# Differential heads: ScalarE copies the four banks, and each head rotates and splits in its lane

## The chip, the cores and the metric

One NeuronCore of a Trainium2 chip runs the whole program in one launch. The metric is the device time of one execution in microseconds (us). Five engines work side by side and meet through semaphores: TensorE (PE) multiplies into the eight banks of PSUM, VectorE (DVE) and ScalarE (ACT) read PSUM and SBUF, GpSimd (POOL) reads SBUF alone, and SyncE (SP) starts transfers from HBM.

## The reference

Two layers of a decoder trunk on 512 tokens of width 2048, in float32. A layer normalises its input, projects it by `w_in`, runs three groups of attention heads beside each other, gates each, and projects the 2048 joined outputs by `w_out`. The change touches the differential heads, of which a layer has four:

```
qa = apply_rope(a_q.reshape(B, S, 4, 2, 64), cos, sin)
ka = apply_rope(a_k.reshape(B, S, 4, 2, 64), cos, sin)
va = a_v.reshape(B, S, 4, 128)
p = softmax(causal(q k^T * 64 ** -0.5))          # two score maps a head
a = p[:, :, 0] - lam * p[:, :, 1]
y_a = rms_norm(a @ va, subln_w, 1e-5) * (1 - lam_init)

apply_rope(x): [x1 * cos - x2 * sin, x2 * cos + x1 * sin]   # halves of 32
```

## The kernel before

Every float32 operand of a large product is split into a rounded part and a remainder (names with `hi`, `h` and `lo`, `l`), and a product is three matmuls: hi by hi, hi by lo, lo by hi. A weight tile of 128 rows comes by DMA into `raw`, ACT rounds it to `whi`, and POOL (during the stages that matter here) subtracts to get `wlo`; there are four slots for such pairs.

A GEMM runs over 16 such tiles (`sweep`), with the four token blocks of 128 in the four PSUM banks `g`. Tiles 0 and 1, and tiles 14 and 15, are taken together, bank by bank; the others one at a time, bank by bank too. Of the differential heads each has a GEMM of its own, with 384 columns (keys 128, queries 128, values 128); a tile of it is 12 matmuls. The next head's GEMM writes the same four banks again.

Attention runs in two **lanes** (class `Lanes`), generators that issue a piece of a head's work after each tile of the GEMM that runs then; a `yield` of a number lets that many modelled microseconds of PE work pass first. `L_SPLIT` is 2.6, `L_ROWS` 3.0, `L_DA` 4.5, `L_RSQRT` 4.0. PE executes in exactly the order in which the program issues; the instructions of the other engines are put in an order by a scheduler at build time, and each engine then keeps to it. `lanes.finish(task)` issues what is left of a task at once, with no GEMM tile between its pieces.

The steps of a head (`da_head`) are, by the names of its tiles: transposes `qT` and `kT` of the rotated queries and keys, scores `sc` for 1, 2, 3 and 4 blocks of keys (shapes 128x128 to 128x512, two maps each), softmax on DVE and ACT into `p`, transposes `pT` of it, products `oT` with the split values `vh`, `vl`, then the norm: column sums `css` on PE, an inverse square root in 11 small DVE instructions (`rsq_u`, `rsub`), its split (`rh`, `rl`) onto two diagonal tiles `dh`, `dl`, and a product `R` on PE that spreads them. A lane has two PSUM banks for all of these in turn.

In the kernel before, the code between two heads' GEMMs reads the banks directly. For each of the four blocks DVE multiplies keys and queries by sine and cosine (`rope`, three instructions that read the bank), adds (two instructions; the keys are written twice, the second time by an ACT copy), ACT writes `vh`, and DVE `vl`, both from the bank. The tables `rtabs` hold sine and cosine already multiplied by the row's norm factor `r_in`.

I call the code after the GEMM of the first, second, third and fourth head boundary 1, 2, 3 and 4 of a layer.

Of the kernel before, what the change touches and what calls it, by code (L numbers as in the profile page):

```python
# [12 lines left out]
F32 = mybir.dt.float32  # L13
F32R = mybir.dt.float32r
I32 = mybir.dt.int32
AF = mybir.ActivationFunctionType
ALU = mybir.AluOpType
AX = mybir.AxisListType

P = 128  # L20
S = 512
NB = S // P
# [86 lines left out]
def trunk(ctx: ExitStack, tc: tile.TileContext, ins, inv_freq, out):  # L109
# [12 lines left out]
    def slot(name, tag, dt=F32, shape=(P, S)):  # L122
        return w2.tile(list(shape), dt, name=name, tag=tag, bufs=SLOTS[tag])
# [7 lines left out]
    lanes = Lanes()  # L131
    V = nc.vector
    A = nc.scalar
# [14 lines left out]
    def split(hi, lo, src, scale=None, behind=False, E=V):  # L148

        if scale is None:  # L150
            late(A.copy(hi, src), behind)  # L151
            E.tensor_tensor(lo, src, hi.bitcast(F32), op=ALU.subtract)  # L152
        else:
            late(A.activation(hi, src, AF.Copy, scale=scale), behind)
            E.scalar_tensor_tensor(lo, src, scale, hi.bitcast(F32), op0=ALU.mult, op1=ALU.subtract)  # L155
# [35 lines left out]
    tabs = [const.tile([P, NB, 64], F32, name=n) for n in ("cos", "sin")]  # L191
# [41 lines left out]
    def rope(dst, src, m, heads, tables, dup=0):  # L233


        co, si = tables
        n, z = heads * 64, dup * 64
        t = slot("rope", "et")
        u = t[:, n:2 * n] if dup else dst
        t = t[:, 0:n]  # L240
        sv, tv, uv = (x.rearrange("p (h d) -> p h d", d=64) for x in (src, t, u))
        V.tensor_tensor(tv[:, :, 0:32], sv[:, :, 32:64],  # L242
                        si[:, m:m + 1, 0:32].broadcast_to([P, heads, 32]), op=ALU.mult)
        V.tensor_tensor(tv[:, :, 32:64], sv[:, :, 0:32],
                        si[:, m:m + 1, 32:64].broadcast_to([P, heads, 32]), op=ALU.mult)
        V.tensor_tensor(uv, sv, co[:, m:m + 1, :].broadcast_to([P, heads, 64]), op=ALU.mult)
        if dup:
            dv = dst[:, 0:2 * z].rearrange("p (h u d) -> p h u d", u=2, d=64)
            V.tensor_tensor(dv[:, :, 0, :], uv[:, 0:dup, :], tv[:, 0:dup, :], op=ALU.add)
            A.copy(dv[:, :, 1, :], dv[:, :, 0, :])  # L250
        if dup < heads:
            V.tensor_tensor(dst[:, 2 * z:], u[:, z:], t[:, z:], op=ALU.add)

    def scaled_tables(r, half, to):

# [99 lines left out]
    def stack_q(lane, tag, tok_tiles, c0):  # L355

        t = bank("qT", lane)
        for m in range(NB):
            transpose(t[:, m * P:(m + 1) * P], tok_tiles[m][:, c0:c0 + P])
        e, o = slot("qe", tag, F32R), slot("qo", tag, F32R)  # L360
        A.copy(e[0:64], t[0:64])
        A.copy(o[64:128], t[64:128])
        V.tensor_tensor(e[64:128], t[0:64], e[0:64].bitcast(F32), op=ALU.subtract)
        V.tensor_tensor(o[0:64], t[64:128], o[64:128].bitcast(F32), op=ALU.subtract)
        return e, o

    def dup_k(lane, tok_tiles, c0, tag="k"):

        t = bank("kT", lane)
        for m in range(NB):  # L370
            transpose(t[:, m * P:(m + 1) * P], tok_tiles[m][:, c0:c0 + P])
        hi, lo = slot("kh", tag, F32R), slot("kl", tag, F32R)
        split(hi, lo, t)
        return hi, lo
# [158 lines left out]
    def layer(l, pre, norms, r_in, start=None):  # L533
# [41 lines left out]
        rtabs = [slot(n, "rtab", shape=(P, NB, 64)) for n in ("rcos", "rsin")]  # L575
        qt = [[None] * NB for _ in range(2)]
        keys = []
        for half in range(2):
            ms = (2 * half, 2 * half + 1)
            ps = gemm_tok(act_block, w_in, [(C_KR, 64), (B_K, 256)], 320, ms=ms,  # L580
                          before=lambda k: fed(half, k))
# [3 lines left out]
            kd = []  # L585
            for t_ps, m in zip(ps, ms):
                d = slot("kd", "rot")
# [6 lines left out]
            if half == 0:  # L594
                c = layer_constants(l)
            ps = gemm_tok(act_block, w_in, [(B_Q, 512)], 512, ms=ms)
# [86 lines left out]
        def spread_r(lane):  # L683
            V.tensor_tensor(r_sq, r_in, r_in, op=ALU.mult)
            d = diagonals(r_in, f"pT{lane}")
            yield L_SPLIT
            t = bank("R", lane)
            spread(t, d)
# [6 lines left out]
        ps = gemm_tok(act_block, w_in, [(B_Q + 512, 512)], 512)  # L695
# [25 lines left out]

        qscale = layer_c.tile([P, NB], F32, name=f"qscale{l}")
        kvscale = layer_c.tile([P, NB], F32, name=f"kvscale{l}")
        R = slot("R", "R")

        def kv_scale(lane, ssum):
            yield L_SPLIT
# [2 lines left out]
            yield L_SPLIT  # L730
            t = bank("R", lane)
            spread(t, d)
            A.copy(R, t)

# [4 lines left out]
        ps = gemm_T(act, w_in, [(C_Q, S)])  # L739
        qh, ql, ssum = latent(ps, c["qnw"])  # L740
        scales = [lanes.add(q_scale, ssum)]
        ps = gemm_T(act, w_in, [(C_KV, S)])
# [4 lines left out]
        ps = gemm_tok(lambda k, m: cut((qh[k], ql[k]), m), w_uq, [(192 * h + 128, 64) for h in range(4)], 256, nk=4)  # L747
        qr = []
        for m in range(NB):
            d = slot("qr", "rot")  # L750
# [11 lines left out]
        for ps in gemm_T(lambda k: (qh[k], ql[k]), w_uq, [(192 * h, 128) for h in range(4)], nk=4):  # L762
            t = (slot("qnh", "gy", F32R), slot("qnl", "gy", F32R))
# [3 lines left out]
        def up_kv(pr, ready):  # L767
# [20 lines left out]
            for j in range(2):  # L788
                t = (slot("knh", "k", F32R), slot("knl", "k", F32R))
                kf = slot("kf", "et")  # L790
                V.tensor_tensor(kf, ps[j], R, op=ALU.mult)
                split(t[0], t[1], kf)
# [6 lines left out]
        def mla_head(lane, h, kn, vv):  # L799
# [3 lines left out]
            for i in range(NB):  # L803
# [8 lines left out]
                if i == 1:  # L812
                    yield L_ROWS
            yield L_MLA
# [4 lines left out]
        kn, vv = up_kv(0, scales + stacks)  # L819
        heads = [lanes.add(mla_head, h, kn, vv) for h in (0, 1)]  # L820
        gate_chunk(C_G, 12)
        kn, vv = up_kv(1, heads)
# [6 lines left out]
        stage = [0] * 5  # L829
        heads_out = [None] * 4  # L830

        def da_head(lane, h, rot, vv):
            yield L_SPLIT
            yield lambda: h == 0 or stage[h - 1] >= 2
            qq = stack_q(lane, f"qE{lane}", rot, 256)
            kk = [dup_k(lane, rot, 0)]
            yield L_SPLIT
            kk.append(dup_k(lane, rot, 128))
            stage[h] = 1
            yield L_SPLIT  # L840
            probs = prob_slots(lane)
            for i in range(NB):
                n = (i + 1) * P
                cc = slice(i * P, (i + 1) * P)
                p1 = slot("p", f"p{lane}")[:, 0:n]
                recs = []
                for u in range(2):
                    t = bank("sc", lane)
                    mm(t[:, 0:n], qq[u][:, cc], kk[u][0][:, 0:n], start=True, stop=False)
                    mm(t[:, 0:n], qq[u][:, cc], kk[u][1][:, 0:n], start=False, stop=True)  # L850
                    recs.append(softmax_rows((probs[i], p1)[u], t[:, 0:n], n, causal[:, S - n:S], 64.0 ** -0.5))
                V.tensor_tensor(recs[1], recs[1], c["nlam"], op=ALU.mult)
                V.tensor_scalar(probs[i], probs[i], recs[0], None, op0=ALU.mult)  # L853
                V.scalar_tensor_tensor(probs[i], p1, recs[1], probs[i], op0=ALU.mult, op1=ALU.add)  # L854
                if i < 3:
                    yield L_ROWS
            stage[h] = 2
            yield L_DA
            o = yield from causal_AV(lane, probs, lambda b: (vv[0][:, b, :], vv[1][:, b, :]))
            sq = slot("sq", f"p{lane}")  # L860
            heads_out[h] = slot("on", "gy")
            A.activation(sq, o, AF.Square)
            A.activation(heads_out[h], o, AF.Copy, scale=c["sub"])
            yield L_ROWS
            ms = sm("ms")
            V.tensor_scalar(ms, col_sums(bank("css", lane), sq), 1.0 / 128, SUB_EPS, op0=ALU.mult, op1=ALU.add)
            d = diagonals(rsqrt(ms, "rsub"), f"pT{lane}")
            yield L_RSQRT + L_SPLIT
            t = bank("R", lane)
            spread(t, d)  # L870
            V.tensor_tensor(heads_out[h], heads_out[h], t, op=ALU.mult)

        das = []
# [4 lines left out]
        for h in range(4):  # L878
            ps = gemm_tok(
                act_block, w_in, [(A_K + 128 * h, 128), (A_Q + 128 * h, 128), (A_V + 128 * h, 128)], 384)  # L880
            if h == 0:
                lanes.finish(*heads)
            if h > 0:
                lanes.finish_until(lambda: stage[h - 1] >= 1)
            if h > 1:
                lanes.finish(das[h - 2])
            rot = []
            vv = (slot("vh", "v", F32R, (P, NB, P)), slot("vl", "v", F32R, (P, NB, P)))
            for m in range(NB):
                d = slot("da_rot", "rot")  # L890
                rope(d[:, 0:384], ps[m][:, 0:256], m, 4, rtabs, dup=2)
                rot.append(d)
                split(vv[0][:, m, :], vv[1][:, m, :], ps[m][:, 256:384], r_in[:, m:m + 1])
            das.append(lanes.add(da_head, h, rot, vv))

        gate_chunk(A_G, 0, lambda k: split_y(k) if k >= 4 else None)

# [65 lines left out]
    r_in = layer_c.tile([P, NB], F32, name="r_in0")  # L963
# [25 lines left out]
    for l in range(1, DEPTH):  # L989
# [1 line left out]


SLOTS = {"gy": 16, "kr": 2, "p0": 4, "p1": 4, "pT0": 2, "pT1": 2, "qE0": 2, "qE1": 2, "k": 4, "v": 4,
         "rot": 6, "rtab": 2, "et": 3, "R": 1, "Rin": 1}
N_RAW = 3
N_SPLIT = 4
L_SPLIT = 2.6
L_ROWS = 3.0
L_SW = 5.0
L_MLA = 7.0  # L1000
L_DA = 4.5
# [29 lines left out]
```

## Time and profile before

| | |
|---|---|
| three runs | 1814.95, 1817.13, 1818.06 us (median 1817.13) |
| profiled execution | 1818.91 us, of which the span of instructions is 1817.1 us |
| PE busy | 1744.7 us, 96% of the span |
| DVE, ACT, POOL busy | 900.4, 816.7, 784.6 us |
| mean granted clock of PE | 0.985 of full speed |

PE is busy nearly all the time, and the matmuls of the program are the floor. What another engine does costs time only where PE waits for it, or where the clock of PE is granted at the lower of its two levels (0.5, that is 1.2 GHz in place of 2.4).

### The profile page before, as it was taken

The page shows a single profiled execution, that of the slowest core. Times are in us where ns is not written, and L with a number is a line of the kernel's source. Part 1 is how long each engine was busy: PE and PEld are TensorE (multiplying, and loading weights), DVE is VectorE, ACT ScalarE, POOL GpSimd, SP SyncE. Part 2 cuts the span into 40 slices and gives each one's busy share as a digit, 9 for nine tenths or more (in the row PEclk, how much of TensorE's full clock was granted, in tenths as well). Part 3 has the DMA queues.
Part 4 walks back from the last instruction along what each step waited for, and adds up shares of the span by engine and source line. Part 5 has one row for each costly group of instructions (what it writes and reads, how often), then busy time and mean ns, then how long its engine had stood idle before and what let it go on. Part 6 is the DMA issues. An engine that isn't in the chain of part 4 may idle for free. (4 is left out here: it accounts for less than half of the span.)

```text
span 1817.1 us, 25547 instructions
## 1 busy us (share of the span) xinstructions
PE 1744.7 (96%) x8832; PEld 1495.9 (82%) x8832; DVE 900.4 (50%) x2374; ACT 816.7 (45%) x1816; POOL 784.6 (43%) x666
## 2 busy tenths in 40 slices
PE   6899999999999999999989999999999999999997
PEld 5778888888999888888777888888889999878875
DVE  7755616653344558301785563364634345572034
ACT  5554525634344445325554453354434343443343
POOL 4344343443433344448434434433434333344663
PEclk9999999999999999999999999999999999999999
DMA  7543232232422224325765323332324222333366
GB/s 198 143 139 93 82 93 71 87 99 70 119 70 76 65 80 127 104 93 186 242 195 154 101 89 93 82 92 71 94 68 122 73 70 65 99 117 108 118 200 206
DMA packets 168673, 202.27 MB, mean 111 GB/s; under 512 B 30800, under 2 KB 92256, under 8 KB 168544
## 3 DMA queue, kind: packets, MB, share of 16 engines
q1 hardware_dynamic: 162160, 190.12, 35.5%
q0 software_dynamic: 3264, 10.51, 1.6%
q8 instruction: 69, 1.13, 0.3%
q10 hardware_dynamic: 3120, 0.01, 0.1%
q14 instruction: 60, 0.49, 0.1%
HBM read 188.02 MB, written 12.58 MB: 110 GB/s over the span
## 5 line engine op out<-in xcount | busy, mean ns | idle before, releaser
L152 POOL TENSOR_TENSOR wlo<-raw,whi 128x512 fp32r<-128x512 f32 (+2 forms) x608 | 753.6, 1246 | 983.5 <-ACT whi L151 943.3
L151 ACT CAST whi<-raw 128x512 fp32r<-128x512 f32 (+3 forms) x704 | 406.3, 581 | 671.1 <-PE g L142 532.7
L142 PE MATMUL g<-wlo,act_hi 128*128 128x512 f32 (+2 forms) x1408 | 525.4, 373 | 28.4 <-DVE wlo L152 26.5
L142 PE MATMUL g<-whi,act_hi 128*128 128x512 f32 (+2 forms) x1408 | 530.3, 377 | 17.1 <-DVE vl L155 13.5
L142 PE MATMUL g<-whi,act_lo 128*128 128x512 f32 (+2 forms) x1408 | 522.1, 371 | 0.8 <-POOL act_lo L152 0.8
L142 PEld LDWEIGHTS g<-wlo,act_hi 128*128 128x128 f32 x1408 | 270.1, 192 | 72.3 <-DVE wlo L152 35.1
L142 PEld LDWEIGHTS g<-whi,act_hi 128*128 128x128 f32 x1408 | 270.2, 192 | 57.5 <-issue 17.6
L142 PE MATMUL g<-act_hi,whi 128*128 128x512 f32 x768 | 311.6, 406 | 5.8 <-DVE vl L155 5.8
L142 PE MATMUL g<-act_hi,wlo 128*128 128x512 f32 x768 | 304.6, 397 | 0.0
L142 PE MATMUL g<-act_lo,whi 128*128 128x512 f32 x768 | 304.4, 396 | 0.0
L142 PEld LDWEIGHTS g<-whi,act_lo 128*128 128x128 f32 x1408 | 269.9, 192 | 35.2 <-POOL act_lo L152 1.0
L142 PEld LDWEIGHTS g<-act_hi,whi 128*128 128x128 f32 x768 | 145.1, 189 | 37.8 <-issue 6.8
L142 PEld LDWEIGHTS g<-act_hi,wlo 128*128 128x128 f32 x768 | 144.9, 189 | 34.9
L142 PEld LDWEIGHTS g<-act_lo,whi 128*128 128x128 f32 x768 | 145.4, 189 | 29.7
L152 DVE TENSOR_TENSOR pTl<-pT,pTh 128x512 fp32r<-128x512 f32 (+2 forms) x112 | 68.2, 612 | 154.6 <-ACT pTh L151 154.5
L152 DVE TENSOR_TENSOR wlo<-raw,whi 128x512 fp32r<-128x512 f32 (+1 forms) x96 | 66.8, 699 | 98.1 <-ACT whi L151 98.1
L923 DVE TENSOR_TENSOR ob<-g,post_norm_w 128x512 f32<-128x512 f32 x32 | 22.1, 691 | 159.7 <-ACT sq L921 159.5
L416 DVE CUSTOM_DVE_ANT_0 p<-sc,causal 128x128 f32<-128x128 f32 (+3 forms) x96 | 45.8, 477 | 57.0 <-PE sc L142 57.0
L151 ACT CAST pTh<-pT 128x512 fp32r<-128x512 f32 (+2 forms) x112 | 58.6, 525 | 26.3 <-PE pT L146 25.3
L418 ACT ACTIVATE p<-p,nm 128x128 f32<-128x128 f32 (+3 forms) x64 | 36.0, 563 | 72.1 <-DVE nm L417 65.0
L146 PE MATMUL pT<-ident,p 128*128 128x128 f32 x384 | 61.1, 275 | 0.3
L242 DVE TENSOR_TENSOR rope<-g,rsin 128x128 f32<-128x128 f32 (+2 forms) x56 | 17.6, 315 | 85.7 <-PE g L142 85.5
(230 smaller groups left out, 2094.4 us busy)
## 6 DMA issues: line engine op xcount, KB each, us to landing
raw<-w_in SPq DMA_DIRECT2D x144, 512.0 KB, 3.7
raw<-w_out SPq DMA_DIRECT2D x96, 512.0 KB, 3.7
raw<-w_in SPq DMA_DIRECT2D x192, 128.0 KB, 2.3
raw<-w_in SPq DMA_DIRECT2D x32, 256.0 KB, 3.2
x<-x SPq DMA_DIRECT2D x16, 256.0 KB, 4.8
y_spill<-gate POOLq DMA_DIRECT2D x16, 256.0 KB, 2.9
raw<-w_ukv SPq DMA_DIRECT2D x8, 512.0 KB, 3.8
yb<-y_spill POOLq DMA_DIRECT2D x16, 256.0 KB, 3.8
```

What stands on the lines that cost most here:

```text
L142: nc.tensor.matmul(out_, a, b, start=start, stop=stop, skip_group_check=True)
L146: nc.tensor.transpose(out_, in_, ident)
L151: late(A.copy(hi, src), behind)
L152: E.tensor_tensor(lo, src, hi.bitcast(F32), op=ALU.subtract)
L242: V.tensor_tensor(tv[:, :, 0:32], sv[:, :, 32:64], si[:, m:m + 1, 0:32].broadcast_to([P, heads, 32]), op=ALU.mult)
L416: V.tensor_tensor_reduce(p, scores, mask, 1.0, -3e38, op0=ALU.add, op1=ALU.max, accum_out=mx)
L418: A.activation(p, p, AF.Exp, bias=nm, scale=scale, accum_out=den)
L923: V.tensor_tensor(ob[n][m], t, post[n], op=ALU.mult)
```

## The change

At a boundary ACT copies each bank (keys, queries, values), multiplied by `r_in`, into one SBUF tile `da_raw` that holds all four blocks; nothing else reads the banks. The lane then rotates queries and keys of all four blocks at once from `da_raw` with the plain tables `tabs` (`rope_parts`), writes `da_q` and two tiles `da_k` with the doubled keys, copies `vh` on ACT and subtracts `vl` on DVE. The lane has two waits `L_ROPE` of 3.0 more, the first ahead of the query transposes. The wait for the head before (now until it has read all of `da_raw`, which has one slot) stands behind `lanes.finish(das[h - 2])`. The tag `rot` has four slots in place of six, and the tile `R` of the latent heads shares `raw`.

```diff
--- before.py
+++ after.py
@@ -251,6 +251,21 @@
         if dup < heads:
             V.tensor_tensor(dst[:, 2 * z:], u[:, z:], t[:, z:], op=ALU.add)
 
+    def rope_parts(src):
+
+        co, si = tabs
+        t = slot("rope", "et").rearrange("p (m c) -> p m c", m=NB)
+        sv, tv = (z.rearrange("p m (h d) -> p m h d", d=64) for z in (src, t))
+
+        def wide(table):
+            d = table.shape[2]
+            return table.rearrange("p m (o d) -> p m o d", o=1).broadcast_to([P, NB, 2, d])
+
+        V.tensor_tensor(tv[:, :, :, 0:32], sv[:, :, :, 32:64], wide(si[:, :, 0:32]), op=ALU.mult)
+        V.tensor_tensor(tv[:, :, :, 32:64], sv[:, :, :, 0:32], wide(si[:, :, 32:64]), op=ALU.mult)
+        V.tensor_tensor(sv, sv, wide(co), op=ALU.mult)
+        return t
+
     def scaled_tables(r, half, to):
 
         mm_ = slice(2 * half, 2 * half + 2)
@@ -721,7 +736,7 @@
 
         qscale = layer_c.tile([P, NB], F32, name=f"qscale{l}")
         kvscale = layer_c.tile([P, NB], F32, name=f"kvscale{l}")
-        R = slot("R", "R")
+        R = slot("R", "raw")
 
         def kv_scale(lane, ssum):
             yield L_SPLIT
@@ -829,14 +844,30 @@
         stage = [0] * 5
         heads_out = [None] * 4
 
-        def da_head(lane, h, rot, vv):
+        def da_head(lane, h, raw, vv):
             yield L_SPLIT
             yield lambda: h == 0 or stage[h - 1] >= 2
-            qq = stack_q(lane, f"qE{lane}", rot, 256)
-            kk = [dup_k(lane, rot, 0)]
-            yield L_SPLIT
-            kk.append(dup_k(lane, rot, 128))
+            rk, rq, rv = raw[:, 0], raw[:, 1], raw[:, 2]
+            A.copy(vv[0], rv)
+            t = rope_parts(rq)
+            qd = slot("da_q", "rot").rearrange("p (m c) -> p m c", m=NB)
+            V.tensor_tensor(qd, rq, t, op=ALU.add)
+            yield L_ROPE
+            t = rope_parts(rk)
+            kd = []
+            for u in range(2):
+                kd.append(slot("da_k", "rot").rearrange("p (m c) -> p m c", m=NB))
+                one, two = (z[:, :, 64 * u:64 * u + 64].rearrange("p m (o d) -> p m o d", o=1)
+                            .broadcast_to([P, NB, 2, 64]) for z in (rk, t))
+                V.tensor_tensor(kd[u].rearrange("p m (o d) -> p m o d", o=2), one, two, op=ALU.add)
             stage[h] = 1
+            qq = stack_q(lane, f"qE{lane}", [qd[:, m] for m in range(NB)], 0)
+            yield L_ROPE
+            kk = [dup_k(lane, [kd[0][:, m] for m in range(NB)], 0)]
+            V.tensor_tensor(vv[1], rv, vv[0].bitcast(F32), op=ALU.subtract)
+            stage[h] = 1.5
+            yield L_SPLIT
+            kk.append(dup_k(lane, [kd[1][:, m] for m in range(NB)], 0))
             yield L_SPLIT
             probs = prob_slots(lane)
             for i in range(NB):
@@ -880,18 +911,16 @@
                 act_block, w_in, [(A_K + 128 * h, 128), (A_Q + 128 * h, 128), (A_V + 128 * h, 128)], 384)
             if h == 0:
                 lanes.finish(*heads)
-            if h > 0:
-                lanes.finish_until(lambda: stage[h - 1] >= 1)
             if h > 1:
                 lanes.finish(das[h - 2])
-            rot = []
+            if h > 0:
+                lanes.finish_until(lambda: stage[h - 1] > 1)
+            raw = slot("da_raw", "raw", shape=(P, 3, NB, P))
             vv = (slot("vh", "v", F32R, (P, NB, P)), slot("vl", "v", F32R, (P, NB, P)))
             for m in range(NB):
-                d = slot("da_rot", "rot")
-                rope(d[:, 0:384], ps[m][:, 0:256], m, 4, rtabs, dup=2)
-                rot.append(d)
-                split(vv[0][:, m, :], vv[1][:, m, :], ps[m][:, 256:384], r_in[:, m:m + 1])
-            das.append(lanes.add(da_head, h, rot, vv))
+                A.activation(raw[:, :, m, :], ps[m][:, 0:384].rearrange("p (k c) -> p k c", k=3), AF.Copy,
+                             scale=r_in[:, m:m + 1])
+            das.append(lanes.add(da_head, h, raw, vv))
 
         gate_chunk(A_G, 0, lambda k: split_y(k) if k >= 4 else None)
 
@@ -991,11 +1020,12 @@
 
 
 SLOTS = {"gy": 16, "kr": 2, "p0": 4, "p1": 4, "pT0": 2, "pT1": 2, "qE0": 2, "qE1": 2, "k": 4, "v": 4,
-         "rot": 6, "rtab": 2, "et": 3, "R": 1, "Rin": 1}
+         "rot": 4, "raw": 1, "rtab": 2, "et": 3, "Rin": 1}
 N_RAW = 3
 N_SPLIT = 4
 L_SPLIT = 2.6
 L_ROWS = 3.0
+L_ROPE = 3.0
 L_SW = 5.0
 L_MLA = 7.0
 L_DA = 4.5
```

How the order moves, at three places of the first layer (the second layer's order is the same there).

PE at boundary 3, where the first head's norm ends. Before, `css` stands inside the GEMM of the third head, followed by the second head's scores for two blocks and more tiles:

```order
L142 MATMUL g<-whi,act_lo 128x384
L142 MATMUL css<-ones_f,sq 128x2 x4
L142 MATMUL sc<-kh,qe 128x256
L142 MATMUL sc<-kl,qe 128x256
L142 MATMUL sc<-kh,qo 128x256
L142 MATMUL sc<-kl,qo 128x256
L142 MATMUL g<-whi,act_hi 128x384
L142 MATMUL g<-wlo,act_hi 128x384
```

and `R` follows three tiles later, still inside that GEMM:

```order
L142 MATMUL g<-wlo,act_hi 128x384
L142 MATMUL g<-whi,act_lo 128x384
L142 MATMUL R<-dh,ones_r 128x512
L142 MATMUL R<-dl,ones_r 128x512
L142 MATMUL g<-whi,act_hi 128x384
L142 MATMUL g<-wlo,act_hi 128x384
```

With the change `css` is issued after the last matmul of the third head's GEMM, and `R` by `lanes.finish`:

```order
L142 MATMUL g<-whi,act_lo 128x384
L142 MATMUL css<-ones_f,sq 128x2 x4
L142 MATMUL sc<-kh,qe 128x256
L142 MATMUL sc<-kl,qe 128x256
L142 MATMUL sc<-kh,qo 128x256
L142 MATMUL sc<-kl,qo 128x256
L142 MATMUL sc<-kh,qe 128x384
L142 MATMUL sc<-kl,qe 128x384
L142 MATMUL sc<-kh,qo 128x384
L142 MATMUL sc<-kl,qo 128x384
L142 MATMUL R<-dh,ones_r 128x512
L142 MATMUL R<-dl,ones_r 128x512
```

Between `css` and `R` eight score matmuls are left, and no tile of a GEMM.

DVE at the same place, from the first instruction that reads `css` to the diagonal tiles that `R` reads. Before there are 24 rows; these are the first twelve (ISA rows are the masked copy with a row maximum, and its read-out):

```order
L866 TENSOR_SCALAR ms<-css 128x4
L160 TENSOR_SCALAR rsq_u<-ms 128x4
L416 ISA p,mx<-sc,causal 128x256
L416 ISA mx 128x1
L161 TENSOR_SCALAR rsub<-rsq_u 128x4
L417 TENSOR_SCALAR nm<-mx 128x1
L163 TENSOR_TENSOR rsq_u<-rsub 128x4
L164 SCALAR_TENSOR_TENSOR rsq_u<-rsq_u,ms 128x4
L165 SCALAR_TENSOR_TENSOR rsub<-rsq_u,rsub 128x4
L163 TENSOR_TENSOR rsq_u<-rsub 128x4
L164 SCALAR_TENSOR_TENSOR rsq_u<-rsq_u,ms 128x4
L419 RECIPROCAL rec<-den 128x1
```

With the change there are 35 rows. The first twelve of them, with three multiplies of the third head's rotation among them:

```order
L897 TENSOR_SCALAR ms<-css 128x4
L160 TENSOR_SCALAR rsq_u<-ms 128x4
L431 ISA p,mx<-sc,causal 128x256
L431 ISA mx 128x1
L161 TENSOR_SCALAR rsub<-rsq_u 128x4
L432 TENSOR_SCALAR nm<-mx 128x1
L163 TENSOR_TENSOR rsq_u<-rsub 128x4
L264 TENSOR_TENSOR rope<-da_raw,sin 128x8x32
L164 SCALAR_TENSOR_TENSOR rsq_u<-rsq_u,ms 128x4
L265 TENSOR_TENSOR rope<-da_raw,sin 128x8x32
L165 SCALAR_TENSOR_TENSOR rsub<-rsq_u,rsub 128x4
L264 TENSOR_TENSOR rope<-da_raw,sin 128x8x32
```

and the last twelve (of the eleven between, two more belong to the rotation, one of them the cosine over 512 columns):

```order
L164 SCALAR_TENSOR_TENSOR rsq_u<-rsq_u,ms 128x4
L434 RECIPROCAL rec<-den 128x1
L431 ISA p,mx<-sc,causal 128x384
L431 ISA mx 128x1
L165 SCALAR_TENSOR_TENSOR rsub<-rsq_u,rsub 128x4
L883 TENSOR_TENSOR rec<-rec,nlam_574 128x1
L432 TENSOR_SCALAR nm<-mx 128x1
L446 CAST rh<-rsub 128x4
L885 SCALAR_TENSOR_TENSOR p<-p,rec 128x256
L447 TENSOR_TENSOR rl<-rsub,rh 128x4
L451 TENSOR_TENSOR dh<-ident,rh 128x512
L451 TENSOR_TENSOR dl<-ident,rl 128x512
```

The rotation's multiplies and the softmax of the scores for three blocks moved ahead of `dh` and `dl`.

ACT at boundary 2. Before, the copies `vh` and `da_rot` of four blocks stand among weight casts and exponentials, each behind a DVE step of the same block:

```order
L154 ACTIVATE vh<-g,r_in_112 128x128
L250 COPY da_rot<-da_rot 128x2x64
L151 CAST whi<-raw 128x384 x2
L154 ACTIVATE vh<-g,r_in_112 128x128
L250 COPY da_rot<-da_rot 128x2x64
L418 ACTIVATE p,den<-p,nm 128x512
L154 ACTIVATE vh<-g,r_in_112 128x128
L418 ACTIVATE p,den<-p,nm 128x512
L250 COPY da_rot<-da_rot 128x2x64
L154 ACTIVATE vh<-g,r_in_112 128x128
L250 COPY da_rot<-da_rot 128x2x64
```

With the change three bank copies stand together, and the fourth behind two weight casts, ahead of the exponentials:

```order
L433 ACTIVATE p,den<-p,nm 128x128 x2
L151 CAST whi<-raw 128x384
L921 ACTIVATE da_raw<-g,r_in_112 128x3x128 x3
L151 CAST whi<-raw 128x384 x2
L921 ACTIVATE da_raw<-g,r_in_112 128x3x128
L433 ACTIVATE p,den<-p,nm 128x256
L851 CAST vh<-da_raw 128x512
L433 ACTIVATE p,den<-p,nm 128x256
```

The copies wait for PE alone, and no DVE step stands between a bank and its release.

## Rows read from the trace of the kernel before

**Rows 1.** The page, section 1: busy us, share of the span, instructions.

```profile
PE 1744.7 (96%) x8832; PEld 1495.9 (82%) x8832; DVE 900.4 (50%) x2374; ACT 816.7 (45%) x1816; POOL 784.6 (43%) x666
```

**Rows 2.** Waits of PE, whole run: who waited for whom, us, times, longest.

```profile
PE g L142 <- DVE wlo L152: 26.5, 18, 4.8
PE g L142 <- DVE vl L155: 19.3, 15, 2.8
```

**Rows 3.** Waits of PE in 490:740, then in 1400:1660 (differential heads, both layers).

```profile
PE g L142 <- DVE vl L155: 9.7, 7, 2.8
...
PE g L142 <- DVE vl L155: 9.0, 6, 2.8
```

**Rows 4.** Timeline of PE in 612.5:619.5, boundary 3 of the first layer.

```profile
616.07 0.41 PE L142 MATMUL g<-whi,act_hi 128*128 128x384 f32 x1 [2.82 <-DVE vl L155]
616.32 0.34 PE L142 MATMUL g<-wlo,act_hi 128*128 128x384 f32 x1
616.50 0.34 PE L142 MATMUL g<-whi,act_lo 128*128 128x384 f32 x1
...
619.03 0.52 PE L142 MATMUL g<-whi,act_lo 128*128 128x384 f32 x1
619.35 0.52 PE L142 MATMUL g<-whi,act_hi 128*128 128x384 f32 x1
```

**Rows 5.** Windows: us, busy by engine, granted clock; five stretches summed, then the start.

```profile
core 0: us, PE busy (x) PEld busy (x) DVE busy (x) ACT busy (x) POOL busy (x), PEclk, DMA share, GB/s
617.30:624.10 6.80, 5.91 (x19) 5.84 (x19) 3.48 (x14) 2.10 (x6) 0.23 (x2) 0.50 0.23 60
...
sum 27.10, PE 24.68 PEld 22.19 DVE 15.98 ACT 7.53 POOL 7.58; mean PE 4.94 PEld 4.44 DVE 3.20 ACT 1.51 POOL 1.52
...
23.20:28.00 4.80, 0.05 (x2) 0.04 (x1) 4.80 (x9) 2.46 (x8) 2.56 (x3) 0.87 0.19 70
28.00:33.60 5.60, 5.60 (x21) 5.60 (x22) 5.29 (x15) 3.91 (x12) 2.76 (x2) 0.50 0.49 123
```

**Rows 6.** ACT reading a bank: duration in ns, min/median/max, by width.

```profile
L154 ACT ACTIVATE vh<-g,r_in x32: 346/368/369, 527.8 to 1563.8; 128x128 fp32r<-128x128 f32 x32
L154 ACT ACTIVATE ch<-g,mla_q_norm_w x8: 682/685/701, 324.9 to 1221.6; 128x512 fp32r<-128x512 f32 x8
```

**Rows 7.** Timeline in 597:606, the first head's norm, from `css` to `R`.

```profile
597.06 0.95 PE L142 MATMUL css<-ones_f,sq 128*128 128x2 f32 x8
597.87 0.36 PE L142 MATMUL sc<-kh,qe 128*128 128x256 f32 x1
598.05 0.16 DVE L866 TENSOR_SCALAR ms<-css 128x4 f32<-128x4 f32 x1 [1.76 <-PE css L142]
...
603.30 0.68 DVE L436 TENSOR_TENSOR dl<-ident,rl 128x512 fp32r<-128x512 f32 x1
...
605.40 0.40 PE L142 MATMUL R<-dh,ones_r 128*128 128x512 f32 x1
605.64 0.39 PE L142 MATMUL R<-dl,ones_r 128*128 128x512 f32 x1
```

**Rows 8.** Instructions on the rotation's tile `rope`: ns min/median/max; `g` is a bank.

```profile
L242 DVE TENSOR_TENSOR rope<-g,rsin x56: 239/281/427, 46.6 to 1562.3; 128x128 f32<-128x128 f32 x32, 128x256 f32<-128x256 f32 x16, 128x96 f32<-128x96 f32 x8
L252 DVE TENSOR_TENSOR q_rot<-q_rot,rope x16: 675/710/1495, 73.2 to 1166.3; 128x512 f32<-128x512 f32 x16
L252 DVE TENSOR_TENSOR qr<-qr,rope x8: 424/880/1564, 389.3 to 1286.9; 128x256 f32<-128x256 f32 x8
```

**Rows 9.** Groups by form in 490:740: count, busy us, mean ns, idle before.

```profile
L416 DVE CUSTOM_DVE_ANT_0 p<-sc,causal 128x512 f32<-128x512 f32 x10 | 6.8, 677 | 0.4 <-PE sc L142 0.4
...
L416 DVE CUSTOM_DVE_ANT_0 p<-sc,causal 128x384 f32<-128x384 f32 x10 | 5.4, 544 | 1.0 <-PE sc L142 1.0
...
L854 DVE SCALAR_TENSOR_TENSOR p<-p,rec 128x512 f32<-128x512 f32 x4 | 3.0, 746 | 0.0
L853 DVE TENSOR_SCALAR p<-p,rec 128x512 f32<-128x512 f32 x4 | 2.9, 724 | 0.0
...
L418 ACT ACTIVATE p<-p,nm 128x512 f32<-128x512 f32 x8 | 5.8, 723 | 9.9 <-DVE nm L417 9.9
```

More of the change, by code (lines that the diff above doesn't have):

```diff
@@ L830, in layer @@
         heads_out = [None] * 4
-        def da_head(lane, h, rot, vv):
+        def da_head(lane, h, raw, vv):
             yield L_SPLIT
             yield lambda: h == 0 or stage[h - 1] >= 2
-            qq = stack_q(lane, f"qE{lane}", rot, 256)
-            kk = [dup_k(lane, rot, 0)]
+            rk, rq, rv = raw[:, 0], raw[:, 1], raw[:, 2]
[11 more added lines that the diff above has]
+                V.tensor_tensor(kd[u].rearrange("p m (o d) -> p m o d", o=2), one, two, op=ALU.add)
+            stage[h] = 1
+            qq = stack_q(lane, f"qE{lane}", [qd[:, m] for m in range(NB)], 0)
[3 more added lines that the diff above has]
+            stage[h] = 1.5
             yield L_SPLIT
-            kk.append(dup_k(lane, rot, 128))
-            stage[h] = 1
+            kk.append(dup_k(lane, [kd[1][:, m] for m in range(NB)], 0))
             yield L_SPLIT
```

## The prediction

> **What bounds the kernel now.** I read the page first: PE is busy for 96% of the span, DVE for 50% [rows 1]. The kernel is bound by the order of PE's work, and a change on DVE and ACT can gain only where PE stands still or runs slowly. So I read the waits of PE next. Two entries are large [rows 2]: 26.5 us for weight splits, which the change does not touch, and 19.3 us for `vl`, the last DVE instruction that reads a GEMM bank. Cut to the differential heads it is 9.7 us in the first layer and 9.0 us in the second [rows 3]; this is PE at the four boundaries, about to write a bank that DVE has not read to the end. The timeline shows the longest, 2.82 us, and what comes after: GEMM matmuls start 0.18 us apart behind the wait and 0.32 us apart a little later [rows 4]. The view by stretches says why: after some of these waits PE's clock is granted at 0.50 of full speed, 1.2 GHz, in five stretches of 27.1 us in all, with 24.7 us of PE work in them [rows 5]. At 0.32 in place of 0.175 us a matmul, 45% of those 24.7 us are lost: 11.2 us.
>
> So the boundaries cost 18.7 us of waits and 11.2 us of slow clock, **30 us**. That is all the change can give back.
>
> **What it removes and adds at the banks.** A block now costs one ACT copy of 384 columns in place of three DVE multiplies, `vl` and an ACT copy. ACT takes 0.37 us for 128 columns and 0.69 us for 512 [rows 6], so 0.58 us for 384 by interpolation. In the last pair of tiles of a GEMM the four banks end 6 x 0.175 = 1.05 us apart, and in the next GEMM's first pair they are wanted 1.05 us apart, the first one 3.15 us after it ended. A copy of 0.58 us each 1.05 us keeps pace. The fourth stands behind two weight casts; even 1.5 us late it is inside its 3.15 us. At boundary 4 exponentials stand among the copies, but the next GEMM has 512 columns there, and wants its banks 6 x 0.235 = 1.4 us apart. I take all 30 us as gained; if ACT were late by an exponential or two, 1 us a boundary would stay.
>
> **What it adds at boundary 3.** The lane is some 6 modelled us longer, so the first head's norm slips from inside the third GEMM to behind it. There `lanes.finish` issues `css`, eight score matmuls and `R` with no tile between, and PE stops at `R` until DVE has written `dl`. Before, `dl` ends 6.92 us after `css` starts (603.98 less 597.06) and `R` starts 1.4 us later still, behind tiles: it waits for nothing [rows 7]. With the change DVE passes 35 instructions and not 24. The eleven added: four rotation multiplies of 256 numbers (from 0.41 us for that width out of a bank, less 0.08 of overlap with the next: 0.33), one of 512 (0.6), a masked copy of 384 (0.54) [rows 8, 9], a combination of 256 (0.4), and four small ones of 0.1 to 0.2: 3.4 us. So `R` starts 6.9 + 3.4 = 10.3 us after `css`. What PE has to do till then is `css` (0.81), scores for two blocks (0.48) and three (0.70): 2.0 us. It stands for **8 us** (7 if POOL, which runs out of tiles meanwhile, stretches less than before; 10 if more).
>
> After the 4.8 us standstill near the start the clock was at 0.50 for all of the 5.6 us that followed [rows 5], which lost 2.5 us. I take 2.4 us behind this one, 1.5 to 3.1. Together 10.4 us a layer, **21 us** in both.
>
> **What it adds at boundaries 2 and 4.** Here the rotation is put on DVE among the softmax of the head before. Between the scores of two blocks (boundary 2) and the transposes `pT` that need the softmax of four, PE has seven tiles (14.7 us), scores (0.7 and 0.9) and three transposes: 16.7 us. DVE has three softmax pairs. For 512 columns that is two masked copies (1.35), a scaling (0.72), a combination (0.75) and some ten small ones of 0.12: 4.0 us; at 0.13 us less for each 128 columns in each of the four, 3.5 and 3.0 us. It has the rotation: four times 0.33 and six of 512 columns at 0.6: 5.0 us. And near the end it stands for the exponentials of 0.72 and 0.19 us, some four times 0.8. Sum 18.7 us at the means of the rows, against 16.7; but the scaling's mean holds delays.
>
> The rotation's price is the open point. The multiplies that read a bank are all between 0.24 and 0.43 us. Instructions on the same tile with both operands in SBUF go from 0.42 to 1.56 us (256 columns, median 0.88) and from 0.68 to 1.50 (512) [rows 8]. With the change all nine rotation instructions and `vl` are of the second kind. The Trainium skill's page "SBUF — State Buffer" (section Who interferes with whom) says that a DVE instruction with two SBUF inputs contends with a GpSimd instruction that reads SBUF, and one with at most one SBUF input does not; the spread in those rows agrees. Bounds: none of the ten is delayed (0), or each by the 0.46 us of the first median (4.6 us). I take 2 us, nearer to the lower end as the median for 512 columns is only 0.04 over its shortest. The wait at boundary 2 then is 18.7 + 2 - 16.7, less some 1 us of delay already in the scaling's mean: **3 us** (0 to 5). At boundary 4 the window is shorter: scores, `R`, two tiles of 24 x 0.235 us twice, 13.6 us in all; two softmax pairs (7.5), the norm's last product (0.6), the rotation (5.0), three waits of 0.8 and some 2 us at the start until the fourth bank copy, which ACT holds behind casts and exponentials. That is 17.5 us, 3.9 too much, and with a part of the same delay **4.5 us** (2.5 to 7). Boundary 1 has no head ahead of it, and boundary 3's standstill lets DVE catch up: nothing there. Together 7.5 us a layer, **15 us** in both; at the lower bounds 5 us, at the upper ones 24 us.
>
> **The sum.** -30 + 21 + 15 = +6 us. The profiled execution took 1818.9 us, 1.8 us above the median of the runs, so 1824.9 there and **1823 us** against 1817.1. Less than 0.2% (3.6 us) either way is about what a measurement can't tell from no change.
>
> **The rivals.**
> *DVE is through in time at boundaries 2 and 4.* Then only the standstill at boundary 3 stands against the gain: -30 + 21 = -9, 1808 us, faster by 0.5%. The point that decides: if the late softmax costs less than 5.4 us in both layers, the kernel is faster by more than 0.2%. For it speaks that the rows' means hold delays that need not recur: at the shortest durations boundary 2 fits into its 16.7 us. Against it, that the waits before, 2.3 us a boundary (18.7 by eight), gave DVE time at these places which it now lacks.
> *The two sides cancel.* Late softmax costs 5.4 to 12.6 us: 1813.5 to 1820.7 us. With no delay of the rotation (5 us) the sum is -4 us, at this rival's edge, and every delay between that and the forecast's leads into it.
> *`R` does not stop PE for long*, because the small chain takes less than DVE's order makes it: with 4 us a layer in place of 8, and no slow clock behind, -30 + 8 + 15 = -7, 1810 us. Against it: an engine keeps to its order, and the rotation stands ahead of `dl`.
> *The change does not free the banks*, since ACT's copies come late behind casts that wait for PE: 1 us at each of eight boundaries, with a slow stretch or two, adds some 11 us to the sum: 1834 us. Nothing in the order speaks for it.
>
> **How the numbers follow.** The forecast (slower, around 1823) 0.47; cancelling 0.22; DVE in time 0.20; `R` short 0.06; banks not free 0.05. The range for 8 in 10 reaches down to DVE in time with the cheaper standstill (1806) and up to the upper bounds at boundaries 2 and 4 with a slow stretch behind each (24 us in place of 15): 1832. The forecast alone lies within 1821 and 1832. Slower 0.52, same 0.22, faster 0.26.
>
> **What would show it.** The waits for `vl` at a GEMM's first matmuls should be gone, 18.7 us, and no low clock should follow a boundary's first tiles but at boundary 3. PE should wait there once a layer for the DVE instruction that writes `dl`, 7 to 10 us, with a clock of 0.50 behind it. Waits of `pT` or `sc` for the softmax (a combination or a masked copy) should appear behind boundaries 2 and 4, 3 and 4.5 us. If the last are absent I am wrong towards faster; if PE still waits for ACT's copies, towards slower. The rotation's instructions should take 0.33 to 0.5 us for 256 numbers and 0.7 to 1.1 for 512.

## The result, and the profile after

The changed kernel took 1834.57 us (median of four runs, 1833.71 to 1836.94) against 1817.6 us of the kernel before in the same comparison: ratio 1.0096, 95% interval 1.0078 to 1.0114. It is 17 us slower. The forecast had the sign, but only +6 us, and the time lies 2.6 us above the range.

The page, section 1, answers to [rows 1]. PE is busy 3.1 us more and stands still 12.8 us more (85.2 us of 1833.0 in place of 72.4 of 1817.1). DVE's time has not grown; ACT has 4.7 us more, POOL 2.6:

```profile
PE 1747.8 (95%) x8832; PEld 1498.1 (82%) x8832; DVE 898.9 (49%) x2262; ACT 821.4 (45%) x1792; POOL 787.2 (43%) x666
```

The waits of PE in the whole run (total us, times, longest), to be held against [rows 2, 3]:

```profile
PE g L142 <- DVE wlo L152: 24.7, 15, 5.5
PE pT L146 <- DVE p L885: 19.2, 6, 4.4
PE sc L142 <- DVE mx L431: 6.5, 8, 1.7
PE R L142 <- DVE dh L451: 5.4, 2, 2.9
...
PE g L142 <- DVE gate L365: 1.9, 2, 1.0
...
PE g L142 <- DVE vl L155: 0.6, 2, 0.3
```

The waits for `vl` of the differential heads, 18.7 us, are gone. Four others (`pT`, `sc`, `R` and the gates) are new or have grown, to 33.0 us in all, half of it in each layer. The timeline of PE in the first layer gives their places. Boundary 2, and the GEMM behind it:

```profile
577.41 0.50 PE L142 MATMUL sc<-kh,qo 128*128 128x512 f32 x1 [0.96 <-DVE mx L431]
585.72 0.33 PE L146 MATMUL pT<-ident,p 128*128 128x128 f32 x1 [0.89 <-DVE p L885]
```

Boundary 3, from `css` to `R`; before, the same two stood 8.3 us apart with GEMM tiles between them [rows 7]:

```profile
609.06 0.95 PE L142 MATMUL css<-ones_f,sq 128*128 128x2 f32 x8
...
610.88 0.44 PE L142 MATMUL sc<-kh,qe 128*128 128x384 f32 x1 [0.29 <-DVE mx L431]
...
613.25 0.69 PE L142 MATMUL sc<-kh,qo 128*128 128x384 f32 x1 [1.75 <-DVE mx L431]
...
616.77 0.77 PE L142 MATMUL R<-dh,ones_r 128*128 128x512 f32 x1 [2.52 <-DVE dh L451]
```

Boundary 4, and then the end of the GEMM of the gates (`gate_chunk(A_G, ...)`), where the fourth head's softmax is wanted:

```profile
679.05 0.48 PE L146 MATMUL pT<-ident,p 128*128 128x128 f32 x1 [4.25 <-DVE p L885]
...
728.01 0.50 PE L142 MATMUL g<-whi,act_hi 128*128 128x512 f32 x1 [0.94 <-DVE gate L365]
...
734.45 0.33 PE L146 MATMUL pT<-ident,p 128*128 128x128 f32 x1 [4.45 <-DVE p L885]
```

With 0.28 at another score of boundary 4 that is, a layer: boundary 2 1.85 us, boundary 3 4.6 (4.9 in the second layer), boundary 4 4.5, the fourth head 5.4.

The slow clock has not gone. The view by stretches, as in [rows 5], shows six stretches at 0.50 in the differential heads (here the first, the last and the sum):

```profile
612.10:622.30 10.20, 6.54 (x18) 5.71 (x19) 10.20 (x40) 2.02 (x6) 0.00 (x0) 0.50 0.16 40
...
1636.10:1639.50 3.40, 3.40 (x9) 2.66 (x9) 1.54 (x3) 0.14 (x1) 0.00 (x0) 0.50 0.42 137
sum 34.00, PE 26.65 PEld 22.26 DVE 22.79 ACT 5.89 POOL 1.81; mean PE 4.44 PEld 3.71 DVE 3.80 ACT 0.98 POOL 0.30
```

45% of the 26.65 us of PE work in them, the share that the prediction worked out, is 12.0 us, where it was 11.2. So -18.7 + 33.0 + 0.8 = +15.1 us; the profiled executions differ by 15.9 (1834.79 less 1818.91).

Last, the instructions that the change put on its new tile (ns min/median/max):

```profile
L921 ACT ACTIVATE da_raw<-g,r_in x32: 560/581/584, 528.2 to 1565.1; 128x384 f32<-128x384 f32 x32
L265 DVE TENSOR_TENSOR rope<-da_raw,sin x16: 399/416/1250, 532.7 to 1569.0; 128x256 f32<-128x256 f32 x16
L862 DVE TENSOR_TENSOR da_k<-da_raw,rope x16: 675/681/1501, 538.6 to 1575.2; 128x512 f32<-128x512 f32 x16
```

The bank copies take 0.58 us, and most of the rotation runs unstretched.

### The profile page after: what moved, and what is told of

Same layout as the page of the kernel before. It is cut to its first block, busy times and chain, and to the rows that moved or that the text cites. A ratio compares the mean times of both kernels' runs of the same rounds, so it can differ in the third digit from the quotient of the medians.

```text
span 1833.0 us, 25365 instructions
## 1 busy us (share of the span) xinstructions
PE 1747.8 (95%) x8832; PEld 1498.1 (82%) x8832; DVE 898.9 (49%) x2262; ACT 821.4 (45%) x1792; POOL 787.2 (43%) x666
## 5 line engine op out<-in xcount | busy, mean ns | idle before, releaser
L146 PE MATMUL pT<-ident,p 128*128 128x128 f32 x384 | 62.0, 275 | 19.2 <-DVE p L885 19.2
L146 PEld LDWEIGHTS pT<-ident,p 128*128 128x128 f32 x384 | 45.2, 141 | 25.8 <-DVE p L885 20.6
```

Of the source, the lines that this page charges most:

```text
L146: nc.tensor.transpose(out_, in_, ident)
```

## The experiments

The change does two things at once: it takes the bank reads from DVE, and it moves every later step of a head on PE, since a lane with two more waits `L_ROPE` is two pieces longer. **Theory A**: the move alone, which lets PE come to a step before DVE is through with the one ahead of it, costs the time. **Rival B**: the rotation from SBUF makes DVE late, by its share of DVE and by contention with POOL. The first three kernels cross the two, with PE's order word for word that of one of the two kernels; the fourth asks about boundary 3.

**Rotation at the boundary.** The lane loses its waits and the rotation; both stand behind the bank copies.

```diff
             for m in range(NB):
                 A.activation(raw[:, :, m, :], ps[m][:, 0:384]..., AF.Copy, scale=r_in[:, m:m + 1])
-            das.append(lanes.add(da_head, h, raw, vv))
+            A.copy(vv[0], rv)
+            t = rope_parts(rq)
...
+            das.append(lanes.add(da_head, h, qd, kd, vv))
```

> The banks are copied by ScalarE as in the changed kernel, but rotation and value split stand in the code at the boundary, for four blocks at once, and the lane has no wait of its own for them; PE's order is word for word that of the kernel before. Theory A (the two waits in the lane make every later step of a head late, and that alone costs the time): the 30 us of the boundaries come back less some 2 us a head where the first transposes now wait for the rotation, about 1800 us (1792 to 1808). Rival B (rotation from SBUF is what makes DVE late, by contention and by its share of DVE's time): about as the changed kernel, 1825 to 1835 us, with waits of pT and sc behind boundaries 2 and 4 still there.

Measured: 1809.01 us, ratio 0.9945 (0.993 to 0.996). A's range was 1 us too low, B is far off. PE doesn't wait at the first transposes, as A had it; it waits 10.3 us for `pTl` and 3.9 for the softmax.

**The kernel before, with late lanes.**

```diff
+            yield 3.0
             qq = stack_q(lane, f"qE{lane}", rot, 256)
+            yield 3.0
             kk = [dup_k(lane, rot, 0)]
```

> The kernel before, its banks read by DVE as ever, with two waits of 3.0 added in the lane of a differential head where the change has its two; PE's order is word for word that of the changed kernel. Theory A: the waits of the changed kernel for R, pT, sc and the gates (33 us) come on top of what the boundaries cost already, 1835 to 1850 us. Rival B: without the rotation from SBUF DVE keeps its time, 1815 to 1823 us.

Measured: 1836.73 us, ratio 1.0094 (1.0079 to 1.0109): the whole loss, with no rotation from SBUF in it, and in A's range. Its waits of PE show the changed kernel's beside what is left of the old ones:

```profile
PE g L142 <- DVE vl L155: 13.9, 10, 4.3
PE pT L146 <- DVE p L856: 9.0, 2, 4.6
PE R L142 <- DVE dh L436: 6.0, 2, 3.0
...
PE sc L142 <- DVE mx L416: 4.2, 6, 1.5
PE g L142 <- DVE gate L350: 1.9, 2, 1.0
```

The waits do not simply add up, as A had them. The late ones are 21.1 us here and 33.0 in the changed kernel; those for `vl` are 13.9 here and 0.6 there. At boundary 4 PE waits 4.28 us for `vl` in this kernel, where the changed one waits 4.25 for the softmax: with the late order DVE is behind there in both.

**The changed kernel without the two waits.** Both lines `yield L_ROPE` are taken out.

> The changed kernel without its two waits of 3.0: rotation and split stay in the lane, ahead of the transposes, and PE's order is word for word that of the kernel before. Theory A: 1797 to 1812 us; against rotation at the boundary the transposes wait longer for it, 1 to 3 us a head. Rival B: 1825 to 1835 us. If the waits were needed to cover the rotation, PE waits for da_q and da_k by 3 us a head or more, 24 us in all, and the time stays near 1825.

Measured: 1806.57 us, ratio 0.993 (0.9915 to 0.9945), in A's range. PE never waits for `da_q` or `da_k`; the waits were not needed to cover the rotation. What is left in the differential heads is 6.6 us in the first layer, as below, and 6.5 in the second:

```profile
PE oT L142 <- DVE pTl L152: 4.6, 3, 3.1
PE pT L146 <- DVE p L883: 2.0, 2, 1.9
```

So the four kernels make a square. By the ratios, in the old order the new handling of the banks wins 10 to 13 us, in the late order nothing (1.0096 against 1.0094); the late order costs 17 us with the old bank reads, and 27 to 30 with the new. The move is enough for the loss, as theory A has it. The waits say where the gain went: in the late order the copies take away 13.3 us of waits for `vl` and put 11.9 us of late waits in their place.

**Values taken in the lane.** `vh` and `vl` are allocated in the lane, and `lanes.finish(das[h - 2])` falls away.

```diff
-            if h > 1:
-                lanes.finish(das[h - 2])
...
+            vv = (slot("vh", "v", F32R, (P, NB, P)), slot("vl", "v", F32R, (P, NB, P)))
             A.copy(vv[0], rv)
```

> The changed kernel with the tiles of split values taken in the lane, so that the code at a boundary need no longer finish the head before the last: css and R of the first head stand inside the fourth GEMM, with tiles between them. Theory A: the wait for R and for the softmax at boundary 3 (4.6 and 4.9 us) and part of the slow clock behind it go, 1818 to 1826 us; the last head's late softmax stays (5.4 us a layer). Rival B: only the place of the wait moves, 1830 to 1836 us.

Measured: 1833.75 us, ratio 1.0078 (1.0062 to 1.0095). Theory A's forecast missed here; the rival's, that the wait only moves, held. The softmax waits at boundaries 3 and 4 are gone. But `R` still comes too soon for DVE inside the fourth GEMM and the gates' (1.47 and 2.98 us in the first layer), `pT` of the last head waits longer (5.7), and `R` of a later head waits 4.4 us more in the output GEMM, at 766.66. With that the first layer waits 17.3 us, where it was 16.3. The view of 490:745, without the last of these:

```profile
PE pT L146 <- DVE p L886: 6.8, 2, 5.7
PE R L142 <- DVE dh L451: 4.4, 2, 3.0
PE sc L142 <- DVE mx L431: 1.7, 2, 1.0
```

A head without `finish` runs later, and so do those behind it. Taking away one place of a late lane moves the wait to the next.

Next I asked what DVE's own work adds to the lateness. **Softmax first**: `tc.high_priority()` around the softmax of these heads and around the split of `pT`.

> The changed kernel with the softmax of the differential heads and the split of pT given priority in the scheduler; PE's order is unchanged. Theory A (a step is late because PE comes to it too early after the one before, whatever DVE does in between): DVE's chain from the scores to the last combination is waited for as before, 1828 to 1836 us. Rival C (DVE has the time, but rotation, SiLU and gate products stand ahead of the softmax in its order): the waits of pT (19.2 us) fall below 10, 1818 to 1826 us.

Measured: 1832.05 us, ratio 1.008 (1.0063 to 1.0097), in A's range and within noise of the changed kernel. Its waits show that here DVE's order only decides who is late:

```profile
PE pT L146 <- DVE p L887: 11.8, 4, 5.1
PE R L142 <- DVE rec L885: 9.7, 2, 5.0
PE sc L142 <- DVE mx L432: 6.0, 6, 1.7
PE g L142 <- DVE gate L365: 5.9, 2, 2.9
```

`pT` gained 7.4 us, most of what rival C had (11.8 us are left, not below 10); `R` lost 4.3 and the gates 4.0.

**The last head in time.**

```diff
-            yield L_ROPE
+            if h < 3:
+                yield L_ROPE
```

> The changed kernel, where the last differential head alone has no waits of 3.0 in its lane; boundaries 1 to 3 keep PE's order. What I left out of the prediction, the last head's softmax that comes late at the end of the gates' GEMM (0.95 + 4.45 us a layer and a slow clock of 3.4 us behind it), should go: 10.8 us of waits and some 3 of the clock, 1820 to 1825 us. If the time stays within 1830 to 1836, the waits only move elsewhere.

Measured: 1825.04 us (1822.14 to 1826.88), ratio 1.0035 (1.0022 to 1.0048): 9.5 us below the changed kernel by the medians, 11 by the ratios. The waits of `pT` fell from 19.2 to 13.8 us and those of the gates from 1.9 to 0.4: 7 us, not the 10.8 expected, since 1.7 us a layer at the fourth head's `pT` stay. The clock gave more than expected: 20.2 us at 0.50 with 14.6 us of PE work in them, in place of 34.0 and 26.65, is 5.4 us. The two slow stretches behind the last head are gone, which is the expected 3 us; the rest comes from shorter ones at boundaries 3 and 4, where the waits are what they were, so it isn't shown to be the edit's.

**No rotation multiplies.**

```diff
-            t = rope_parts(rq)
+            t = rq
...
-            t = rope_parts(rk)
+            t = rk
```

> The changed kernel without the six multiplies by sine and cosine of each differential head (left out: the rotation itself; the adds and all transposes stay, on unrotated numbers); PE's order is unchanged. It sizes the rotation's share in the waits of the changed kernel. Theory A: the last head's waits (5.4 us a layer) stay as they are, having no rotation beside them; those of boundaries 2 to 4 (11 us a layer) lose at most the rotation's own 2.6 us a boundary, in all 6 to 14 us: 1820 to 1829 us. Rival B (rotation and its contention with GpSimd make the softmax late): they go altogether, with the slow clock behind them, 1805 to 1815 us.

Measured: 1822.58 us, ratio 1.0025 (1.0014 to 1.0036), in A's range. The last head's waits stay (0.94 and 4.43). Boundary 2's are gone, the `pT` of boundary 4 waits 2.54 in place of 4.25, and `R` waits longer, not less:

```profile
PE pT L146 <- DVE p L885: 13.9, 4, 4.4
PE R L142 <- DVE dh L451: 6.8, 2, 3.4
...
PE sc L142 <- DVE mx L431: 4.8, 6, 1.9
```

The waits are 5.6 us less (27.4 against 33.0), and the stretches at 0.50 are 20.4 us with 15.3 us of PE work, in place of 34.0 and 26.65, which gives back 5.1 us more. So in the late order leaving out the multiplies is worth 12 us, about what the copies gain in the old order. Even without them this kernel is slower than before. Rival B names a part: 12 of the 27 to 30 us that the late order costs with the new handling. It doesn't carry the loss, since the rotation from SBUF stands in the first and third kernels too, and they are faster than before. What the multiplies cost in the old order was not measured.

**One wait.** The first of the two lines `yield L_ROPE` is taken out.

> The changed kernel with only the second of its two waits (between the query transposes and the first key transposes). The first head's css and R then stand inside the third GEMM with tiles between them, as before, while the softmax of the later heads is still late by one step. Theory A: the wait for R and for the scores at boundary 3 (4.7 us a layer) and the slow clock behind it go, and half or more of the late softmax: 1809 to 1820 us, between the kernel without waits and the changed one. If only the whole slip decides, 1830 us or more; if PE now waits for the rotated queries, 1 to 3 us a head show at the first transposes.

Measured: 1825.93 us, ratio 1.0039 (1.0024 to 1.0055), 6 us more than A's range. `R` no longer waits, as expected. The late softmax and gates outside boundary 3 are not halved, they grew from 11.8 to 13.2 us in the first layer; in the whole run:

```profile
PE pT L146 <- DVE p L884: 22.1, 6, 4.4
...
PE g L142 <- DVE gate L365: 4.4, 2, 3.2
...
PE sc L142 <- DVE mx L431: 1.7, 2, 0.8
```

So one wait of 3.0 already puts later steps where DVE is not in time. That this is because a lane gets its turn only once a tile was not tried.

The last two build on the order without waits. **Without waits, softmax first**: the priority of the fifth kernel on the third.

> The kernel without waits in the lane, with the softmax of the differential heads and the split of pT given priority. Its remaining waits are pTl (4.6 us a layer) and pT (1.9 us a layer), where DVE has the rotation ahead of them. Theory A gives no change there, 1804 to 1809 us; rival C gives up to 10 us, 1796 to 1803 us.

Measured: 1804.99 us, ratio 0.9926 (0.9908 to 0.9944). It is A's range, and within noise of the kernel without the priority (0.993). The priority did not bring `pTl` forward: at boundary 3 its operand `pTh` is written by 620.21, and six instructions of the rotation and the value split still start on DVE before it, the first at 620.56:

```profile
619.63 0.58 ACT L151 CAST pTh<-pT 128x512 fp32r<-128x512 f32 x1
...
626.35 0.68 DVE L152 TENSOR_TENSOR pTl<-pT,pTh 128x512 fp32r<-128x512 f32 x1
```

**Keys doubled by ACT**, on top of the last:

```diff
-                V.tensor_tensor(kd[u].rearrange(...), one, two, op=ALU.add)
+                V.tensor_tensor(kd[u][:, :, 0:64], rk[:, :, 64 * u:64 * u + 64], t[:, :, 64 * u:64 * u + 64], op=ALU.add)
+                A.copy(kd[u][:, :, 64:128], kd[u][:, :, 0:64])
```

> The kernel without waits in the lane, softmax first, and each key written once by DVE and a second time by ScalarE, as in the kernel before. DVE's two adds of 512 columns (0.68 us each, up to 1.5 stretched) become two of 256. The waits that are left (pT 1.9 us a layer at boundary 2, pTl 3.1 us a layer at boundary 3) fall by 0.5 to 1.5 us each: 1800 to 1804 us. If ScalarE's copies come late to the key transposes instead, 1805 to 1810.

Measured: 1797.26 us (1795.74 to 1800.74), ratio 0.9874 (0.9851 to 0.9897), 21 us faster than before in the same comparison, and by the ratios some 40 faster than the changed kernel. That is 3 us below the expected range. `pTl` waits half as long as without this edit (3.9 against 7.8 us in the whole run), `pT` as long, not less. The clock, which the expectation left out, makes up the rest: in the differential heads of the two layers together one stretch at 0.50 is left of three, 3.4 us, in the second; the view by stretches over the first layer's gives a granted clock of 1.00:

```profile
490.00:745.00 255.00, 250.74 (x1393) 232.17 (x1392) 148.00 (x387) 117.51 (x259) 110.93 (x97) 1.00 0.34 95
```

## Why the prediction was wrong

*The banks.* Right in what it removes: no wait for `vl` at a boundary is left, and ACT's copies keep pace at 0.58 us each, as interpolated. In the old order the copies gain, which the first and third kernels show.

*The slow clock.* It was counted as gone (-11.2) except behind boundary 3 (+4.8), -6.4 in all. It cost 12.0, +0.8: a slow stretch stands behind boundary 3 as forecast, but also behind boundary 4's wait and the fourth head's, which the sum gave none. This term was off by 7 us.

*Boundary 3.* The step was right, its size not: 4.6 and 4.9 us in place of 8 a layer, 6.5 us too much in both. I had set `R` 10.3 us behind `css` by adding eleven instructions to the chain before; it came after 7.7. Three things differ. The eleven took 3.0 us from start to start, not 3.4. `R` starts behind `dh` at 616.77, and not behind `dl`, which ends at 617.23. And the chain itself got shorter: the norm's 14 small instructions (`ms`, the inverse square root, `rh` and `rl`) took 3.4 us from start to start before and 1.7 now. Some 0.8 us of that is that they no longer follow right upon each other (0.2 us apart at 599.39 to 600.18 before; now others run between them). The rest was stretching that didn't recur: POOL subtracted weight tiles at 597.90 to 598.91 and 601.34 to 602.36 before, and stands still from 611.34 to 624.43 now. The prediction allowed 1 us for that, beside its 8. Two instructions of the kernel before, left out of [rows 7]:

```profile
598.24 0.70 DVE L160 TENSOR_SCALAR rsq_u<-ms 128x4 int32<-128x4 int32 x1
...
601.38 0.99 DVE L165 SCALAR_TENSOR_TENSOR rsub<-rsq_u,rsub 128x4 f32<-128x4 f32 x1
```

and the same two of the changed kernel:

```profile
610.24 0.17 DVE L160 TENSOR_SCALAR rsq_u<-ms 128x4 int32<-128x4 int32 x1
...
615.20 0.16 DVE L165 SCALAR_TENSOR_TENSOR rsub<-rsq_u,rsub 128x4 f32<-128x4 f32 x1
```

That is 1.4 us, of which 0.5 came back at another (`rsub` of L161, 0.62 in place of 0.16). Besides, PE's work up to `R` took 3.1 us, not 2.0, part of it at the slow clock. The kernel without multiplies can't size their share here: there `R` starts 8.3 us behind `css` (607.74 to 616.03), no sooner, but the rotation's adds and `vl` (2.4 us) stand ahead of `dh` in the multiplies' place (1.9 us).

*Boundaries 2 and 4.* 1.85 and 4.5 us, against 3 and 4.5 predicted. The rival that DVE is in time there is out. The multiplies are part of the cause: without them the wait at boundary 2 is gone and that of boundary 4 is 1.7 us shorter.

*The step that failed* is "Together 7.5 us a layer", the sum over late softmax: it went through the four boundaries and stopped there, with two places, and there is a third. The last head slips too, and its softmax falls into the end of the gates' GEMM, where DVE has SiLU and gate products to do. The timeline of DVE there in the changed kernel, from the first masked copy over 512 columns to the last combination:

```profile
724.06 0.68 DVE L431 CUSTOM_DVE_ANT_0 p<-sc,causal 128x512 f32<-128x512 f32 x1
...
724.66 2.03 DVE L152 TENSOR_TENSOR act_lo<-gate,act_hi 128x512 fp32r<-128x512 f32 x2
...
729.61 0.68 DVE L932 TENSOR_TENSOR gate<-on,gate 128x512 f32<-128x512 f32 x1
...
732.65 1.75 DVE L885 SCALAR_TENSOR_TENSOR p<-p,rec 128x512 f32<-128x512 f32 x1
```

It takes 10.3 us, of which the two splits `act_lo` and six instructions on gates are some 5.6. PE, whose `pT` starts at 734.45, waits 4.45 us for it and 0.94 for a bank of the gates: 10.8 us in both layers. The kernel with the last head in time got about 10 us back. The prediction followed PE's new order up to boundary 4 and not to the end of the last lane.

The terms together: +6 as forecast, +7.2 for the clock, -6.5 at boundary 3, -2.3 at boundary 2, +10.8 for the last head, make the +15.1 of the first section. That the forecast came as near as it did is in part luck: two terms that were 8.8 us too large hid half of the 18.0 us that the clock and the last head came to beyond it.

What stays open: which of DVE's instructions ahead of `dh` could be moved to let `R` start sooner, and why the clock is low for 10.2 us at boundary 3 in the first layer and 6.8 in the second.

## What to carry to other kernels

Where one engine runs in a fixed order, a wait added in one lane moves all that follows in this lane: go through its steps to the last one, and ask at each what the serving engine does at that time now. Try a rearrangement of engines and a shift of order apart, in a kernel that has the old order with the new engines; here the first won 10 to 13 us in the old order and nothing in the late one, and the second lost 17 to 30. When taking away one wait only moves it, look for a lane that is late; the serving engine's priorities did not mend that here.

## What the runs showed of the hardware

The rotation's DVE instructions, with both operands in SBUF, cost two prices, by what POOL did. In the kernel without waits POOL subtracts four weight tiles from 615.55 to 620.14. Of the multiplies that start in that time two below take 1.2 us over 256 columns and one 1.5 over 512; the one that starts behind it takes 0.41:

```profile
615.55 4.59 POOL L152 TENSOR_TENSOR wlo<-raw,whi 128x384 fp32r<-128x384 f32 x4 [3.94 <-ACT whi L151]
...
616.87 1.23 DVE L265 TENSOR_TENSOR rope<-da_raw,sin 128x256 f32<-128x256 f32 x1
618.02 1.23 DVE L264 TENSOR_TENSOR rope<-da_raw,sin 128x256 f32<-128x256 f32 x1
619.18 1.51 DVE L266 TENSOR_TENSOR da_raw<-da_raw,cos 128x512 f32<-128x512 f32 x1
620.61 0.41 DVE L265 TENSOR_TENSOR rope<-da_raw,sin 128x256 f32<-128x256 f32 x1
```

The Trainium skill's page "SBUF — State Buffer", section Who interferes with whom, says that such an instruction contends with a GpSimd instruction that reads SBUF. These rows agree, and give the price, a factor of 2 to 3 (0.68 us is the short time over 512 columns, at 613.58 of the changed kernel, where POOL stands still). The multiply of L265 has a median of 0.416 us in the changed kernel and 1.203 in this one, which I had not expected: its place in time decides.

The prediction gives another rule of the Trainium skill's page "SBUF — State Buffer", section Who interferes with whom (an instruction with at most one SBUF input does not contend), without the page's exception, the 2-port perf modes. The rows show a case of contention with one SBUF input: `rsub` of L161 reads one SBUF tile, and took 0.62 us at 610.74 of the changed kernel, until POOL's subtraction ended at 611.34, and 0.16 at 599.19 of the kernel before, where POOL stood still. Which mode it ran in no run shows.
